# A Trainium2 decoder layer in which the sums of the second feed-forward's weight quarters are made at other places

## The chip, the cores and the metric

The kernel runs on one core of one Trainium2 chip. The metric is the time of one execution on the device in microseconds (us); lower is better. The time before is the median of three runs. A profile is one execution taken by the hardware profiler; its times count from the first instruction. The engines are TensorE (PE; PEld is its weight load), VectorE (DVE), ScalarE (ACT), GpSimd (POOL) and SyncE (SP, which here issues DMAs alone).

## The reference, cut to what matters

One layer works on x of 512 tokens by 1024, in float32. It has three steps, each with an RMS norm before and behind it and a residual.

```python
x = x + 0.5 * rms_norm(swiglu_ffn(rms_norm(x, norm_pre[0]), ffn1_w_in, ffn1_w_out), norm_post[0])
x = x + rms_norm(token_mixer(rms_norm(x, norm_pre[1]), ...), norm_post[1])
x = x + 0.5 * rms_norm(swiglu_ffn(rms_norm(x, norm_pre[2]), ffn2_w_in, ffn2_w_out), norm_post[2])

def swiglu_ffn(x, w_in, w_out):                  # w_in 1024 x 5632, w_out 2816 x 1024
    gate, up = jnp.split(x @ w_in, 2, axis=-1)
    return (jax.nn.silu(gate) * up) @ w_out
```

The token mixer projects to eight heads: four of HGRN2 (a gated linear recurrence) and four of mLSTM (scores of queries and keys under a causal mask and a decay, with a running maximum). Then it projects back.

## The kernel before, in words

**Precision.** Every large product is made of two-part numbers: a weight is cast to fp32r by ScalarE (L279, the high part), VectorE subtracts that from the weight (L281, the low part), and TensorE runs three matmuls, high by high, high by low and low by high. A split weight lies in one of four places (`WBUF`); TensorE frees a place when it has used it.

**Fewer products.** The feed-forwards use a scheme of seven products in place of eight for a 2 by 2 blocked product. It needs sums of blocks. For the input weights these are made in SBUF (L295, VectorE and some on GpSimd). For the output weights of most tiles (`QUARTERED`: eight in the first half of the output columns, five in the second, thirteen in all) the sums of a tile's quarters are made in DRAM, ahead of use, by `sums_ahead` (L862): SP copies three quarters of the weight tile into a DRAM tile (L868 to L870, 128, 128 and 256 KB), and then GpSimd issues three accumulating DMAs, DRAM to DRAM (L873): one of 256 KB, which adds the remaining quarter to two places, and two of 128 KB, each of which reads what the one before it wrote. Each waits for the landing of what it reads. The finished tile is later loaded by SP like any weight (L242, `raw<-f2sums`).

**Where the sums are made.** `sums_due` (L876) makes a list of tiles for one feed-forward and chosen halves; `make_sums` (L879) begins the next tile of the list (SP's copies) and moves every tile already begun one step on (one of GpSimd's DMAs). Calls of `make_sums` stand at fixed points of the program:

- the mixers (`mixer`, L1671): list = the eight tiles of the second feed-forward's first half. Calls: one for each of four convolution jobs (`job_f`, L1046) and one for each of eight weights of the jobs `hi` and `mv` (`job_t`, L1064). Twelve calls.
- the input products (`ffn_in`, L782): for the second feed-forward a list of five tiles (second half), one call for every tenth product from the twentieth on (`EVERY`), five calls. The first feed-forward has a list of all its thirteen tiles and a call for every fifth product, ten calls.
- the output products (`ffn_out`, L885): a call after every other tile of the first half of the columns, six in all. They begin the first feed-forward's last three tiles and finish the second's fifth.

**What sets the order.** The order of each engine's instructions is fixed when the program is built, and each engine runs its own list in order; between engines there are only semaphores. SP's copies are put behind the last weight load that was recorded before them. GpSimd's accumulating DMAs stand in GpSimd's list between its other work, and an instruction that waits for a landing holds all that is behind it on GpSimd.

**The mixers.** Long projections are cut into small jobs, and `fill(n)` puts n pieces of them between the steps of the recurrences, so that TensorE always has something. After the jobs `hi` and `mv` come `hgrn_states` (L1394) and `mlstm_scores` (L1528). For each mLSTM head, `mlstm_head` (L1504) does this: TensorE spreads a row (L1489), VectorE and ScalarE make the decay e (L1511 to L1514), GpSimd puts zeros above the diagonal (`affine_select`, L1515), TensorE makes the scores in a PSUM bank (L1523), and VectorE multiplies both into pT (L1525), which frees the bank. Before the masks, GpSimd clears a state tile C (L1548). The heads are staggered by one.

**The output products.** `ffn_out` computes the first 512 columns (half 0) with eight quartered tiles (42 matmuls, two weights each: the weight itself and its sums) and three plain ones (48 matmuls), then half 1 with five quartered tiles and six plain ones. Between the halves, `post0` takes sums of squares of half 0, on ScalarE and GpSimd (L436, L437). The last rows are normalized, added and stored (L492, L1807). The program ends with a drain on every engine and a barrier (L1861).

Of the kernel before, what the change touches and what calls it, by code (L numbers as in the profile page):

```python
# [11 lines left out]
ALU = mybir.AluOpType  # L12
# [72 lines left out]
PLACES, LATER = {2: 1, 4: 2, 6: 0, 8: 3}, {7: (2, 3)}  # L85

AGAIN, ROWS = (10,), (18, 19, 20, 21)
EVERY = 5, 10

# [25 lines left out]
class Layer:  # L117
# [663 lines left out]

    def ffn_in(self):  # L782

        self.sums_due("f2" if self.second else "f1", (1,) if self.second else (0, 1))
        for n, (p, t) in enumerate(ORDER2[len(HEADS2) :] if self.second else ORDER[len(HEADS) :]):
            if n > 14 and n % EVERY[self.second] == 0:
                self.make_sums()
            with self.behind(*(self.c22 if p == "p3" and self.second else ())):
                self.feed()
            self.c22 = []  # L790
            self.lag()
            self.prod(p, t)
            self.after(p, t)
            if t == PAIRS - 1 and p in ("p3", "p7"):
                self.hs.append(self.h_tile(len(self.hs)))
        self.feed()
        self.lag()
# [64 lines left out]
    def sums_ahead(self, f, h, k2):  # L862

        nc, to = self.nc, self.sums_of[f, h, k2]
        w = (self.ffn1_w_out, self.ffn2_w_out)[f == "f2"][0]
        q = w[k2 * 2 * P : (k2 + 1) * 2 * P, h * 512 : (h + 1) * 512].rearrange("(k p) (c f) -> p k c f", p=P, f=QUARTER)
        with self.behind(self.loaded):
            nc.sync.dma_start(to[:, 0], q[:, 0, 1])  # L868
            nc.sync.dma_start(to[:, 1], q[:, 1, 0])
            nc.sync.dma_start(to[:, 2:], q[:, 1])  # L870
        yield
        for a, b, v in ((0, 2, q[:, 0, :1].broadcast_to([P, 2, QUARTER])), (2, 3, to[:, :1]), (3, 4, to[:, 2:3])):
            nc.gpsimd.dma_start(to[:, a:b], v, accum_op=ALU.add)  # L873
            yield

    def sums_due(self, f, halves):  # L876
        self.ahead, self.making = deque(k for k in self.sums_of if k[0] == f and k[1] in halves), []

    def make_sums(self):  # L879

# [4 lines left out]
    def ffn_out(self, gpost_row, scale, after, trans, head):  # L885
# [3 lines left out]
        nc, mm = self.nc, self.nc.tensor.matmul  # L889
# [6 lines left out]
        def more(n):  # L896
            while count[0] < min(n, len(seq)):
                half, k2 = seq[count[0]]
                count[0] += 1
                if k2 in QUARTERED[half]:  # L900
                    if k2 not in kept:
                        stay = k2 in QUARTERED[1]
                        kept[k2] = self.h_quarters(k2, PLACES.get(k2)), self.h_sums(k2, stay)
                    a, f = kept[k2]
                    made.append((a, self.s_tile(f)))
                elif half and k2 in AGAIN:
                    made.append(again.popleft())
                else:
                    made.append((self.h_tile(k2, self.x_place(*LATER[k2]) if half and k2 in LATER else None), None))
                    if not half and k2 in AGAIN:  # L910
                        again.append(made[-1])
# [21 lines left out]
        def quartered(C, M, a, s, begin):  # L933

            quarter = lambda t, j: [self.quarters(t[:, b])[j] for b in range(2)]
            A, S = (lambda j: [a[0][j], a[1][j]]), (lambda j: [s[0][j], s[1][j]])
            w = self.pull()
            product(M["p1"], A(1), quarter(w, 1), begin)
            product(C[1][1], A(3), quarter(w, 3), False)
            product(C[1][0], S(3), quarter(w, 2), False)  # L940
            self.drop(w)
            v, at = self.pull(), (1, 0, 2, 3)
            product(M["p7"], S(0), quarter(v, at[0]), begin)
            product(M["p5"], S(1), quarter(v, at[1]), begin)
            product(M["p6"], S(2), quarter(v, at[2]), begin)
            product(C[0][1], A(2), quarter(v, at[3]), False)
            self.drop(v)

        def common(M, t):

            p1, q, x, y = t
            nc.scalar.copy(p1, M["p1"])
            tt(q, M["p5"], p1, ALU.subtract)
            tt(q, M["p6"], q, ALU.add)
            tt(x, q, M["p7"], ALU.subtract)
            tt(y, M["p5"], x, ALU.subtract)
            return {(1, 1): p1, (1, 0): q, (0, 0): x, (0, 1): y}

        def add(C, T, u):
            for v in range(2):  # L960
                tt(C[u][v], C[u][v], T[u, v], ALU.add)

        def pieces(C, i):
            c = slice(QUARTER * (i // 2), QUARTER * (i // 2 + 1))
            return [(C[i % 2][v][:, c], slice(QUARTER * v, QUARTER * (v + 1))) for v in range(2)]


        with self.behind(*([self.loaded] if self.second else [])):
            g = self.gain("gpost", gpost_row)
        n = 0  # L970
        for half in range(2):
            C = [[self.ps() for _ in range(2)] for _ in range(2)]
            M, T, left = None, None, len(QUARTERED[half])
            for m, k2 in enumerate(OUT[half][: PAIRS - LAST * half]):
                more(n + 2)
                h, sums = made.popleft()
                if sums:
                    begin = M is None
                    if begin:
                        M = {p: self.ps() for p in ("p1", "p5", "p7", "p6")}  # L980
                    quartered(C, M, h, sums, begin)
                    left -= 1
                    if left == 0:
                        T = common(M, [self.hf[:, j, :] for j in ROWS] if half else [self.st("c") for _ in range(4)])
                else:
                    w = self.pull()
                    more(len(seq) if half and m == PAIRS - LAST - 1 else n + 3)
                    for i in (0, 2, 1, 3):
                        for v in range(2):
                            plain(C, w, h, i, v, m == 0)  # L990
                        if i > 1 and T and m == PAIRS - 1:
                            add(C, T, i % 2)
                    self.drop(w)
                n += 1
                if half == 0 and n % 2:
                    self.make_sums()
                if n == 1:
                    self.prod("p4", PAIRS - 1)
                    self.after("p4", PAIRS - 1)
                self.lag()  # L1000
            if half == 0:
                ys = [self.post0(pieces(C, i), g, scale) for i in range(NT)]
                self.holes()
        ws = []
# [41 lines left out]
    def job_f(self, name, then):  # L1046

        w, ps = self.pull(), self.ps()
        if name[0] == "c":
            self.make_sums()  # L1050
        for k in range(ND):
            self.in_k(ps, w, k, [(0, HALF), (HALF, T)])
            if k < ND - 1:
                yield
        self.drop(w)
        then(ps)
        self.got.add(name)
        yield
# [368 lines left out]
    def job_rows(self):  # L1427

        ps = self.ps()[:100]
        for k in range(ND):  # L1430
            for n in range(2):
                for m in range(2):
                    v = slice(HALF * m, HALF * (m + 1))
                    self.nc.tensor.matmul(
                        ps[:, v], self.gw[:, k, :], self.xop(k, n, HALF * m, HALF * (m + 1)),
                        start=k + n + m == 0, stop=k == ND - 1 and n == 1, skip_group_check=True,
                    )
            if k % 2 == 1 and k < ND - 1:
                yield
        self.z = self.mb.tile([36, 2, T], F32, tag="tmp", bufs=1, name="z")  # L1440
        self.nc.scalar.copy(self.z[:, 1], ps[64:100])
        self.nc.vector.scalar_tensor_tensor(self.z[:, 0], ps[0:36], self.gb, self.z[:, 1], op0=ALU.add, op1=ALU.add)
        self.got.add("rows")
        yield
# [226 lines left out]
    def mixer(self):  # L1671
        nc, tc = self.nc, self.tc
        self.got, self.jobs = set(), deque()
        self.sums_due("f2", (0,))
        with tc.tile_pool(name="ma", bufs=1) as ma:
            self.vh = ma.tile([P, NT, NH, P], F32, name="vh")
            self.vm = ma.tile([P, NT, NH, 129], F32, name="vm")
# [187 lines left out]
```

## Time and profile before

| | us |
|---|---|
| median of three runs | 937.68 |
| lowest and highest run | 935.62, 940.22 |
| the profiled execution's time | 936.0 |
| its span, first to last instruction | 934.3 |
| TensorE busy | 922.8 |
| VectorE busy | 759.2 |
| GpSimd busy | 179.5 |

The span of 934.3 us has these stages: the first feed-forward to about 340, the mixers to about 597, the input products of the second feed-forward to 813, its output products to 927 and a tail. A row of a timeline is start, length, engine, line, operation, out<-in and, in brackets, how long the engine had been idle and what ended that. A row of a chain of waits is start, length and what the time went to. A row of windows is the stretch and its length, then for TensorE, its weight loads, VectorE, ScalarE and GpSimd the busy time (and instructions), then the granted TensorE clock, the share of the DMA engines and GB/s. A row of a DMA list is destination<-source, queue, count, size and the median time from issue to landing.

### The profile page before, as it was taken

Reading aid. Unit: us, or ns where it says so; the run is one execution under the profiler, and the core shown is the slowest. Engines: PE = TensorE matmul, PEld = TensorE weight load, DVE = VectorE, ACT = ScalarE, POOL = GpSimd, SP = SyncE. Lnnn points to the kernel's source line nnn. Section 1 sums busy time; section 2 is a strip of 40 time slices with the busy share of each in tenths; the row PEclk is TensorE's granted clock in tenths of the full one; section 3 lists DMA queues with packets and bytes.
Section 4 is the critical chain, followed back from the end, with each engine's and each line's share of the span. In section 5 each row is a group of like instructions: output and inputs, shape, how many; then the busy total and the mean of one; then the engine's idle time right before and its main releaser. Section 6 shows DMA issues by size and latency. Waiting matters only on the chain.

```text
span 934.3 us, 18295 instructions
## 1 busy us (share of the span) xinstructions
PE 922.8 (99%) x7435; PEld 887.7 (95%) x7435; DVE 759.2 (81%) x980; ACT 521.5 (56%) x751; POOL 179.5 (19%) x250
## 2 busy tenths in 40 slices
PE   9999999999999999999999999999999999999996
PEld 7999999999999999998888887899999999999996
DVE  6899988889887786698766555799899889988883
ACT  7646455557566457956523345594445545756641
POOL 3531112211111045222230310313010010100001
PEclk9999999999999999999999999999999999999999
DMA  9255778766996234477742125253376556467522
GB/s 315 70 152 143 187 206 194 193 147 160 241 276 215 81 98 123 121 176 160 170 87 63 45 90 175 88 166 93 97 192 171 150 159 198 132 193 224 175 74 91
DMA packets 116494, 142.28 MB, mean 152 GB/s; under 512 B 7189, under 2 KB 89657, under 8 KB 116410
## 3 DMA queue, kind: packets, MB, share of 16 engines
q1 hardware_dynamic: 101562, 126.95, 43.8%
q0 software_dynamic: 14560, 13.64, 11.2%
q8 instruction: 58, 0.95, 0.4%
q10 hardware_dynamic: 288, 0.52, 0.2%
q14 instruction: 26, 0.21, 0.1%
HBM read 138.99 MB, written 29.36 MB: 180 GB/s over the span
## 4 chain that ended last, share of the span: by engine, by line
PE 54%; DVE 5%; issue 2%; DMA 2%; POOL 1%; ACT 1%; DVEq 0%; POOLq 0%; ACTq 0%
PE ps L602 14%; PE ps L928 7%; PE ps L532 6%; PE ps L920 5%; PE ps L185 5%; PE ps L187 5%; PE ps L186 5%; DVE w L281 2%; PE ps L1342 2%; DMA raw<-in_ffn_w_in_dram 2%; DVE raw L295 1%; PE ps L347 1%; POOL raw L295 1%; PE ps L542 1%; PE ps L1523 0%
## 5 line engine op out<-in xcount | busy, mean ns | idle before, releaser
L279 ACT CAST w<-raw 128x1024 fp32r<-128x1024 f32 x244 | 249.6, 1029 | 195.8 <-PE ps L602 85.5
L281 DVE TENSOR_TENSOR w<-raw,w 128x1024 fp32r<-128x1024 f32 x244 | 297.5, 1222 | 32.8 <-ACT w L279 31.5
L602 PE MATMUL ps<-xq,w 128*128 128x256 f32 x2016 | 237.3, 277 | 0.0
L602 PEld LDWEIGHTS ps<-xq,w 128*128 128x128 f32 x2016 | 232.9, 188 | 0.1
L602 PE MATMUL ps<-sq,w 128*128 128x256 f32 x1512 | 178.2, 276 | 2.2 <-DVE ps L621 1.8
L602 PEld LDWEIGHTS ps<-sq,w 128*128 128x128 f32 x1512 | 174.3, 188 | 3.2 <-issue 2.0
L295 DVE TENSOR_TENSOR raw<-raw,raw 128x1024 f32<-128x1024 f32 x72 | 89.8, 1251 | 11.8 <-DMA raw<-in_ffn_w_in_dram 10.3
L920 PE MATMUL ps<-w,hs 128*128 128x256 f32 x768 | 91.2, 276 | 0.0
L920 PEld LDWEIGHTS ps<-w,hs 128*128 128x128 f32 x768 | 88.9, 188 | 0.0
L185 PE MATMUL ps<-w,xq 128*128 128x512 f32 x192 | 78.0, 407 | 0.1
L928 PE MATMUL ps<-w,hs 128*128 128x256 f32 x624 | 75.0, 276 | 0.0
L186 PE MATMUL ps<-w,xq 128*128 128x512 f32 x192 | 74.9, 391 | 0.0
L187 PE MATMUL ps<-w,xq 128*128 128x512 f32 x192 | 74.8, 391 | 0.0
L928 PEld LDWEIGHTS ps<-w,hs 128*128 128x128 f32 x624 | 72.7, 188 | 0.0
L532 PE MATMUL ps<-xq,w 128*128 128x256 f32 x480 | 55.7, 277 | 0.0
L532 PEld LDWEIGHTS ps<-xq,w 128*128 128x128 f32 x480 | 54.9, 188 | 0.5 <-issue 0.5
L814 ACT CAST hs<-hf 128x1024 fp32r<-128x1024 f32 x34 | 35.8, 1053 | 34.2 <-PE ps L928 22.3
L815 DVE TENSOR_TENSOR hs<-hf,hs 128x1024 fp32r<-128x1024 f32 x34 | 41.5, 1221 | 11.9 <-ACT hs L814 11.5
L873 POOL DMA_DIRECT2D f1sums<-f1sums x26 | 22.8, 879 | 111.7 <-DMA f1sums<-in_ffn_w_out_dram 53.1
L185 PEld LDWEIGHTS ps<-w,xq 128*128 128x128 f32 x192 | 36.1, 188 | 8.5 <-issue 0.9
L187 PEld LDWEIGHTS ps<-w,xq 128*128 128x128 f32 x192 | 36.0, 188 | 8.1 <-DVE xq L354 0.3
L873 POOL DMA_DIRECT2D f2sums<-in_ffn_w_out_dram x13 | 17.3, 1333 | 137.3 <-DMA f2sums<-in_ffn_w_out_dram 137.3
(262 smaller groups left out, 1201.6 us busy)
## 6 DMA issues: line engine op xcount, KB each, us to landing
raw<-in_ffn_w_in_dram SPq DMA_DIRECT2D x98, 512.0 KB, 4.9
raw<-in_ffn_w_out_dram SPq DMA_DIRECT2D x44, 512.0 KB, 4.5
raw<-in_w_mix_in_dram SPq DMA_DIRECT2D x28, 512.0 KB, 4.1
raw<-f1sums SPq DMA_DIRECT2D x13, 512.0 KB, 7.5
raw<-f2sums SPq DMA_DIRECT2D x13, 512.0 KB, 4.5
raw<-in_w_mix_out_dram SPq DMA_DIRECT2D x8, 512.0 KB, 4.3
f1sums<-in_ffn_w_out_dram SPq DMA_DIRECT2D x26, 128.0 KB, 4.4
f1sums<-in_ffn_w_out_dram SPq DMA_DIRECT2D x13, 256.0 KB, 5.5
```

The costliest lines, as they stand in the source:

```text
L185: mm(ps, sh, mh, start=start, stop=False, **kw)
L186: mm(ps, sh, ml, start=False, stop=False, **kw)
L187: mm(ps, sl, mh, start=False, stop=stop, **kw)
L279: nc.scalar.copy(hi, raw)
L281: self.low = nc.vector.tensor_tensor(lo, raw, hi.bitcast(F32), op=ALU.subtract)
L295: (nc.vector if late else nc.gpsimd).tensor_tensor(o, o, c, op=ALU.add)
L532: mm(ps[:, u0:u1], w[:, a, k, :], self.xop(k, b, u0, u1), start=k + n + m == 0, stop=k == ND - 1 and n == 2, skip_group_check=True,)
L602: self.nc.tensor.matmul(ps[:, c], wb[b][:, k, v], left[d][:, k, :], start=first and a + n + k == 0, stop=n == 2 and k == KH - 1, skip_grou ...
L815: self.nc.vector.tensor_tensor(lo, src, hi.bitcast(F32), op=ALU.subtract)
L873: nc.gpsimd.dma_start(to[:, a:b], v, accum_op=ALU.add)
L920: mm(out, a[kk][:, i * P : (i + 1) * P], w[:, b, kk, QUARTER * v : QUARTER * (v + 1)], start=begin and c == kk == n == 0, stop=kk == 1 and ...
L928: mm(ps[:, QUARTER * c : QUARTER * (c + 1)], A[a][:, c], B[b], start=begin and c == n == 0, stop=n == 2, skip_group_check=True,)
```

## The change

The list of the mixers gets ten tiles instead of eight (`AHEAD`), and the job of the gate rows (`job_rows`, between the convolutions and `hi`) gets a call of `make_sums` of its own, so that there are thirteen calls. The second feed-forward's input products make none. The remaining three tiles are begun in the first half of its output products, by the first three of the six calls there. Behind the last accumulating DMA a drain is issued on GpSimd. (The other edit of `job_f` names the same four jobs as before.)

```diff
-EVERY = 5, 10
+EVERY, AHEAD = 5, 10
...
     def ffn_in(self):
-        self.sums_due("f2" if self.second else "f1", (1,) if self.second else (0, 1))
+        if not self.second:
+            self.sums_due("f1")
...
-            if n > 14 and n % EVERY[self.second] == 0:
+            if n > 14 and n % EVERY == 0 and not self.second:
                 self.make_sums()
...
-            nc.gpsimd.dma_start(to[:, a:b], v, accum_op=ALU.add)
+            self.summed = nc.gpsimd.dma_start(to[:, a:b], v, accum_op=ALU.add)
...
-    def sums_due(self, f, halves):
-        self.ahead, self.making = deque(k for k in self.sums_of if k[0] == f and k[1] in halves), []
+    def sums_due(self, f, n=None, done=0):
+        self.ahead, self.making = deque([k for k in self.sums_of if k[0] == f][done:n]), []
...
     def ffn_out(self, gpost_row, scale, after, trans, head):
...
+        if self.second:
+            self.sums_due("f2", done=AHEAD)
...
             if half == 0:
+                if self.second:
+                    with self.behind(self.summed):
+                        nc.gpsimd.drain()
                 ys = [self.post0(pieces(C, i), g, scale) for i in range(NT)]
...
     def job_f(self, name, then):
-        if name[0] == "c":
+        if name in ("conv0", "conv1", "conv2", "conv3"):
             self.make_sums()
...
     def job_rows(self):
         ps = self.ps()[:100]
+        self.make_sums()
...
     def mixer(self):
-        self.sums_due("f2", (0,))
+        self.sums_due("f2", AHEAD)
```

In the built programs TensorE, VectorE and ScalarE have the same instructions in the same order before and after. On GpSimd, the six accumulating DMAs of the ninth and tenth tile stand behind those of the eighth and ahead of the clearing of C (L1548) and the four masks (L1515). Among the mixers' tiles, the sixth's first accumulation comes directly behind the fifth's, and the seventh's first one ahead of the sixth's third. The drain stands behind the last accumulating DMA and ahead of `post0`'s first instruction on GpSimd. On SP, the sixth tile's copies follow the fifth's without a weight load between, and those from the seventh to the tenth are each one weight load earlier than that count would put them; the copies of the last three tiles stand among the loads of the output weights, the first of them behind the load of the gains.

## The prediction

> **What bounds the kernel now.** Three views, in this order: the page's first part, TensorE's own waits, and the windows of single stages.
>
> ```profile
> span 934.3 us, 18295 instructions
> ...
> PE 922.8 (99%) x7435; PEld 887.7 (95%) x7435; DVE 759.2 (81%) x980; ACT 521.5 (56%) x751; POOL 179.5 (19%) x250
> ```
>
> ```profile
> PE ps L602 <- DVE ps L621: 1.8, 1, 1.8
> ```
>
> ```profile
> 753.00:775.00 22.00, 20.10 (x175) 19.74 (x174) 18.43 (x20) 8.30 (x11) 2.84 (x3) 1.00 0.66 180
> 813.00:827.00 14.00, 14.00 (x126) 14.00 (x125) 12.67 (x18) 6.14 (x10) 1.66 (x2) 1.00 0.87 224
> 827.00:870.00 43.00, 43.00 (x382) 43.00 (x381) 36.74 (x42) 27.21 (x33) 0.00 (x0) 1.00 0.64 199
> 927.20:931.00 3.80, 0.00 (x0) 0.00 (x0) 1.84 (x3) 0.31 (x2) 0.81 (x2) 1.00 0.21 78
> 931.00:934.30 3.30, 0.00 (x0) 0.00 (x0) 0.00 (x0) 0.00 (x0) 0.00 (x0) 0.51 0.18 70
> ```
>
> TensorE (first column after the length) is busy in 922.8 of 934.3 us. The profiled execution took 936.0 us, 1.7 around its span and 1.7 under the median of the runs shown (937.68); every sum below is made against 936.0. In the whole second feed-forward TensorE has one wait worth a line, 1.8 us, and the window 753 to 775 shows it: 20.10 busy of 22.00. So there is little to win, about 2 us there and something at the end of the kernel, and anything that holds TensorE in its long busy stretches costs its full length. I therefore looked for what the moved DMAs could hold up.
>
> **The change, part by part.** TensorE, VectorE and ScalarE keep their instructions in the same order. What moves is on SP (three copies per tile) and on GpSimd (three accumulating DMAs per tile).
>
> *1. Two more tiles on GpSimd's queue in the mixers.* The GpSimd timeline, with the length of the instruction and in brackets what it waited for:
>
> ```profile
> 429.87 1.49 POOL L873 DMA_DIRECT2D f2sums<-in_ffn_w_out_dram  x1
> ...
> 437.43 1.52 POOL L873 DMA_DIRECT2D f2sums<-in_ffn_w_out_dram  x1
> ...
> 445.57 0.81 POOL L873 DMA_DIRECT2D f2sums<-f2sums  x1 [4.38 <-DMA f2sums<-in_ffn_w_out_dram]
> ...
> 450.11 1.49 POOL L873 DMA_DIRECT2D f2sums<-in_ffn_w_out_dram  x1
> ...
> 463.20 1.49 POOL L873 DMA_DIRECT2D f2sums<-in_ffn_w_out_dram  x1
> ...
> 474.60 1.48 POOL L873 DMA_DIRECT2D f2sums<-in_ffn_w_out_dram  x1
> 481.00 0.85 POOL L873 DMA_DIRECT2D f2sums<-f2sums  x1 [4.92 <-DMA f2sums<-in_ffn_w_out_dram]
> 484.44 0.94 POOL L873 DMA_DIRECT2D f2sums<-f2sums  x1 [2.59 <-ACT vm L1696]
> 485.42 1.40 POOL L1548 MEMSET C<- 128x1548 f32 x1
> 486.77 0.83 POOL L1515 TENSOR_SCALAR_AFFINE_SELECT e<-e 128x512 f32<-128x512 f32 x1
> ```
>
> ```profile
> 448.01 0.49 SPq L868 DMA_DIRECT2D f2sums<-in_ffn_w_out_dram  x1
> ```
>
> ```profile
> f2sums<-in_ffn_w_out_dram POOLq DMA_DIRECT2D x13, 256.0 KB, 6.1
> f2sums<-f2sums POOLq DMA_DIRECT2D x26, 128.0 KB, 4.1
> ```
>
> SP has issued the eighth tile's copies at 448.01; GpSimd reaches that tile at 474.60. The fifth tile begins at 429.87, the sixth at 437.43. So the chain on GpSimd sets the pace: the second accumulation of a tile reads what the first wrote, the third what the second wrote, and GpSimd, in order, waits through 6.1 and 4.1 us of landing (medians of the DMA issues). Tiles begin at 450.11, 463.20 and 474.60, which is 13.1 and 11.4 us each; the last takes 9.84 from its first accumulation to its third and would free the queue after about 10.4. Behind its third accumulation, at once, stand the clearing of C and the first causal mask of the mLSTM scores (L1515): this queue is already as late as those two.
>
> The new order puts two tiles in front of them. At 11.4 and 10.4 that is 21.8 us. Something comes back: the fifth and sixth tile now issue their first accumulations together, and the seventh's goes ahead of the sixth's third, so that part of a wait such as 437.43 to 445.57 (8.1 us) lies beside another. But the same DMA engines serve both, so I take back 5.3 of the 8.1. The last third accumulation moves by 16.5, from 484.44 to 500.9. Bounds: 20.8 (twice 10.4) less the whole 8.1 gives 497.1; twice 13.1 with nothing back gives 510.6.
>
> Who waits for the mask:
>
> ```profile
> 488.60 0.68 DVE L1525 SCALAR_TENSOR_TENSOR pT<-ps,e 128x512 f32<-128x512 f32 x1
> ```
>
> ```profile
> 493.45 1.16 PE L1523 MATMUL ps<-qk 64*128 64x128 f32 x8
> ```
>
> VectorE's product pT of the first head reads the mask and frees the PSUM bank into which TensorE's third group of score products (493.45) goes. From the last third accumulation to the mask's end are 3.16 us (484.44 to 487.60); pT takes 0.68, and I allow 0.2 for two handovers: 4.04. TensorE's group can start at 500.9 + 4.04 = 504.9 instead of 493.45, and TensorE stands still for **11.5 us** (7.7 to 21.2). VectorE stands too, and with it the next splits and ScalarE's exponential of the third head, but up to four weights lie ready for TensorE, so nothing more is late when pT is done. Nothing later takes the 11.5 us back: after the start, the view of TensorE's waits has only the 1.8 us above.
>
> *2. The clock after such a gap.* After the last matmul the granted clock (third number from the end in the windows above) is still 1.00 up to 931.0 and 0.51 from there: 3.8 idle us, and it falls. At the start:
>
> ```profile
> 1.56 1.22 PE L181 MATMUL ps<-ident 128*128 128x128 f32 x4 [1.56 <-POOL ident masks.py:199]
> ...
> 6.42 1.65 PE L181 MATMUL ps<-ident 128*128 128x128 f32 x6
> 7.93 1.82 PE L347 MATMUL ps<-ident,xn 128*128 128x128 f32 x8
> 9.59 0.61 PE L181 MATMUL ps<-ident 128*128 128x128 f32 x4
> 10.07 1.32 PE L347 MATMUL ps<-ident,hf 128*128 128x128 f32 x8
> ```
>
> Six transposes from 6.42 to 7.93 are 0.25 us each, four from 9.59 to 10.07 are 0.12: half speed up to about 9.4, that is for 7.8 us from the first matmul at 1.56. A gap of 11.5 us is long enough for the clock to fall, and the way back costs between 0 and 3.9 us (half of 7.8). I take **2.0**, the middle. The Trainium skill ("TensorE: Matmul & The Clock Gate", Part 1, the HAM clock gate) says that one idle window of about 3.4 us halves the clock and about 3.4 us of work restores it; both rows agree in kind, and by its window the way back would cost 1.7 as an estimate, the sum 0.3 less.
>
> *3. No sums beside the second input products.*
>
> ```profile
> 749.31 0.51 SPq L868 DMA_DIRECT2D f2sums<-in_ffn_w_out_dram  x1
> ```
>
> ```profile
> 653.42 5.21 DMA raw<-in_ffn_w_in_dram
> ...
> 753.62 6.21 DMA raw<-in_ffn_w_in_dram
> ...
> 771.80 3.00 PE ps L602 x24
> ```
>
> ```profile
> raw<-in_ffn_w_in_dram SPq DMA_DIRECT2D x98, 512.0 KB, 4.9
> ```
>
> The chain of waits passes through a weight load of 6.21 us at 753.62, issued behind a tile's copies (749.31), and ends in TensorE's wait before 771.80. The same sort of load took 5.21 at 653.42, with no sums near, and 4.9 in the median. One us or so off the load, and less company for VectorE's next loads, takes most of the 1.8 us: **-1.5**, between 0 (VectorE is late by its own work) and -2.0. The other three tiles of this stage cost TensorE nothing now.
>
> *4. Three tiles beside the first half of the output products* in place of the end of one. The first feed-forward already runs like that:
>
> ```profile
> 240.00:283.00 43.00, 43.00 (x382) 43.00 (x381) 37.81 (x47) 27.04 (x37) 8.01 (x11) 1.00 0.95 275
> ```
>
> ```profile
> 280.60 0.81 POOL L873 DMA_DIRECT2D f1sums<-f1sums  x1 [5.91 <-DMA f1sums<-f1sums]
> 281.17 0.48 POOL L437 TENSOR_SCALAR col<-col 128x1 f32<-128x1 f32 x1
> ```
>
> There the DMA engines are 0.95 busy (0.64 in the same stage of the second, 827 to 870 above), and TensorE works 43.00 of 43.00 us. So these three tiles cost **0**; what they have taken up by then is the queue: the last accumulation is issued right ahead of the sums of squares (L437).
>
> *5. The drain.*
>
> ```profile
> L1861 POOLq DRAIN  x3: 34/102/5506, 928.0 to 934.0; - x3
> ...
> L1861 SPq DRAIN  x3: 7/7/7, 932.2 to 933.8; - x3
> ```
>
> At the end GpSimd's drain lasts 5.5 us, from 928.0 to 933.5, while SP, last of the others, is through its own at 932.2. The next drain, with no DMA between, takes 0.1. If the long one is the price of the software DMAs before it, it is now paid between the halves, and the end waits for SP: **-1.3**. If not, 0. The early one stands, by the rows of part 4, at the moment when the sums of squares are due, and can hold the two instructions of ScalarE that wait for GpSimd there, and a cast behind them, for up to 5.5 us. Up to four split weights cover that, so I cost it at 0, and at +2 if they don't.
>
> Sum: 936.0 + 11.5 + 2.0 - 1.5 + 0 - 1.3 = 946.7, about **947** (on the median of the runs it would be 948.4).
>
> **The rivals.**
>
> *A. The chain fits (not slower).* The mechanism is the same queue: if the last third accumulation is issued before 493.45 - 4.04 = 489.4, TensorE waits for nothing, and only the gains stay: 936.0 - 1.5 - 1.3 = 933.2. It needs the two tiles to cost 5.0 us net instead of 16.5, say 8.1 back and 6.5 us each. Against it: landing alone is 6.1 + 4.1 in the median, and no tile of these took under 9.8. The Trainium skill ("DMA: Bandwidth & Descriptors", Anatomy of one DMA, SWDGE path) gives about 2.0 us plus bytes over 436 GB/s, so an estimated 2.6 and 2.3 us for these two sizes, and by it the queue would be on time; the medians 6.1 and 4.1 speak against that, and these move data from HBM to HBM. Chance 0.14.
>
> *B. The drain between the halves holds TensorE.* For it: GpSimd, ScalarE's casts and TensorE hang on each other there. Against it: the cover. Price 2 to 4 us, a drain less what the cover takes: about 950. Chance 0.08.
>
> *C. The change does not bring what it is made of:* the wait before 771.80 is VectorE's own work (for it: 18.43 busy of 22.00 us from 753 to 775; against it: the load that stood before), and the last drain lasts as long as now. Then 946.7 + 2.8 = 949.5. Chance 0.10.
>
> **How the numbers follow.** The forecast has 0.68. Its own range comes from the queue's bounds, 7.7 to 21.2, of which the upper end needs the slowest tile twice: 936.0 + 7.7 - 2.0 - 1.3 = 940.4 up to about 936.0 + 17 + 2 - 1.5 = 953.5. B and C lie inside for the most part; towards A I reach down to 938. Outside is most of A and a little above 954. A measurement here tells about 0.5% (4.7 us) from no change. Faster by more than that would need more than all gains together (2.0 + 1.3): 0.04. Within it lie A and the forecast with a chain near its lower bound: 0.15. Slower: 0.81.
>
> **What would show it.** In the profile after: GpSimd's third accumulation of the tenth tile near 501 (497 to 511), the clearing of C right behind it, and a TensorE gap of some 11 us before a group of L1523, near 493, released by VectorE's L1525; a stretch under full clock behind it; no wait before the matmuls that were at 771.80 (all times there later by the gap); GpSimd's last drain short. The forecast is wrong if the clearing of C stands before 490, or if TensorE waits inside the output products.

## The result and the profile after

The kernel after takes 945.12 us (median of 6 runs, 943.48 to 949.19) beside 937.80 for the kernel before in the same sessions: a ratio of 1.0087, 95% interval [1.0068, 1.0105] (the two medians alone give 1.0078). It is slower by 7.3 us between the medians, by 8.2 by the ratio. Its profiled execution took 945.62 us, 9.6 more than that of before (936.0), and it is these 9.6 us that the traces can be asked for. The lines of the code have moved: L873 is L874 now, L1515 is L1522, L1523 is L1530, L1525 is L1532, L1548 is L1555, L1861 is L1868.

The page's first part, and TensorE's own waits:

```profile
span 943.9 us, 18290 instructions
...
PE 926.2 (98%) x7435; PEld 891.2 (94%) x7435; DVE 758.2 (80%) x980; ACT 522.1 (55%) x751; POOL 180.2 (19%) x250
```

```profile
PE ps L1530 <- DVE pT L1532: 8.5, 1, 8.5
...
PE ps L602 <- DVE ps L621: 0.7, 1, 0.7
```

One wait is new, 8.5 us before a group of score products, and the wait in the input products went from 1.8 to 0.7. GpSimd's timeline shows where the 8.5 us come from; the first row is the two first accumulations that are now issued together, the second is the eighth tile's third, and from 478.47 on it is the ninth and the tenth tile. (The two that are issued together belong to the tiles that the text above calls the fifth and the sixth. Counted in the list they are the fourth and the fifth, which changes none of the times.)

```profile
431.49 2.65 POOL L874 DMA_DIRECT2D f2sums<-in_ffn_w_out_dram  x2
...
477.94 0.81 POOL L874 DMA_DIRECT2D f2sums<-f2sums  x1 [2.67 <-DMA f2sums<-f2sums]
478.47 1.48 POOL L874 DMA_DIRECT2D f2sums<-in_ffn_w_out_dram  x1
484.54 0.85 POOL L874 DMA_DIRECT2D f2sums<-f2sums  x1 [4.59 <-issue]
487.90 0.81 POOL L874 DMA_DIRECT2D f2sums<-f2sums  x1 [2.50 <-DMA f2sums<-f2sums]
488.43 1.48 POOL L874 DMA_DIRECT2D f2sums<-in_ffn_w_out_dram  x1
495.87 0.85 POOL L874 DMA_DIRECT2D f2sums<-f2sums  x1 [5.96 <-DMA f2sums<-in_ffn_w_out_dram]
499.25 0.81 POOL L874 DMA_DIRECT2D f2sums<-f2sums  x1 [2.52 <-DMA f2sums<-f2sums]
500.10 1.39 POOL L1555 MEMSET C<- 128x1548 f32 x1
501.45 1.24 POOL L1522 TENSOR_SCALAR_AFFINE_SELECT e<-e 128x512 f32<-128x512 f32 x2
```

The rows of VectorE and TensorE that follow from the mask at 501.45, one fence for each engine:

```profile
502.14 0.69 DVE L1532 SCALAR_TENSOR_TENSOR pT<-ps,e 128x512 f32<-128x512 f32 x1 [13.82 <-POOL e L1522]
```

```profile
493.96 0.39 PE L187 MATMUL ps<-w,xq 128*128 128x512 f32 x1
502.88 2.08 PE L1530 MATMUL ps<-qk 64*128 64x128 f32 x8 [8.53 <-DVE pT L1532]
```

VectorE sat idle 13.82 us for the mask, TensorE 8.53 us for VectorE. The same eight score products took 1.16 us before and take 2.08 here: the clock has fallen. The windows of single stages (length, then TensorE, its weight loads, VectorE, ScalarE, GpSimd; granted clock, DMA share, GB/s) show that and the stages behind it:

```profile
494.35:502.88 8.53, 0.00 (x0) 0.00 (x0) 0.74 (x2) 0.00 (x0) 4.25 (x5) 0.67 0.24 33
502.88:505.50 2.62, 2.62 (x10) 2.30 (x11) 2.62 (x8) 1.57 (x2) 0.64 (x1) 0.50 0.00 0
505.50:508.00 2.50, 2.50 (x8) 2.01 (x7) 2.00 (x6) 0.73 (x2) 0.99 (x1) 0.61 0.10 11
508.00:515.00 7.00, 7.00 (x37) 5.29 (x36) 3.58 (x9) 3.12 (x6) 0.00 (x0) 1.00 0.21 72
763.00:785.00 22.00, 21.18 (x185) 20.82 (x184) 19.09 (x20) 9.00 (x11) 0.00 (x0) 1.00 0.44 137
837.00:880.00 43.00, 43.00 (x382) 43.00 (x381) 36.16 (x42) 26.86 (x31) 7.38 (x8) 1.00 0.91 263
```

TensorE's granted clock is 0.50 for 2.62 us and 0.61 in the mean of another 2.50: 2.62 x 0.50 + 2.50 x 0.39 = 2.3 us lost. From 508 on it is at full speed. In the output products it is fully busy although the DMA share there went from 0.64 to 0.91.

The drains, first those at the end, then the new one:

```profile
L1868 POOLq DRAIN  x3: 38/93/656, 938.9 to 943.6; - x3
L1868 SPq DRAIN  x3: 7/7/7, 943.1 to 943.4; - x3
```

```profile
L1007 POOLq DRAIN  x1: 6561/6561/6561, 878.0 to 878.0; - x1
```

From the start of GpSimd's last drain to the end of the span it is 943.9 - 938.9 = 5.0 us; before it was 934.3 - 928.0 = 6.3. One more difference has nothing to do with the change, the same transposes at the start of the kernel as in the rows shown of before:

```profile
9.69 1.06 PE L181 MATMUL ps<-ident 128*128 128x128 f32 x4
10.55 1.91 PE L347 MATMUL ps<-ident,hf 128*128 128x128 f32 x8
12.28 5.94 PE L602 MATMUL ps<-xq,sq 128*128 128x256 f32 x48
```

Four transposes take 1.06 us here and took 0.61, the next eight 1.91 and 1.32: in this execution the clock rose later, and what follows stands 0.8 to 0.9 us later from there on. Of the ten profiles of this case, that of before has the earliest start: the first matmul of L542, behind the first feed-forward, is at 339.73 there, at 340.56 in that of after, and between 339.94 and 341.10 in the others.

The sum of what was read: 8.5 (wait) + 2.3 (clock) - 1.1 (idle time in the input products: 1.90 of 22 us before, 0.82 here) - 1.3 (end) + 0.9 (start) = 9.3 of the 9.6 us.

### The profile page after: what moved, and what is told of

Read it like the earlier page. It is cut to its first block, busy times and chain, and to the rows that moved or that the text cites. A ratio compares the mean times of both kernels' runs of the same rounds, so it can differ in the third digit from the quotient of the medians.

```text
span 943.9 us, 18290 instructions
## 1 busy us (share of the span) xinstructions
PE 926.2 (98%) x7435; PEld 891.2 (94%) x7435; DVE 758.2 (80%) x980; ACT 522.1 (55%) x751; POOL 180.2 (19%) x250
## 4 chain that ended last, share of the span: by engine, by line
PE 36%; DVE 5%; issue 3%; DMA 3%; POOL 2%; ACT 1%; DVEq 0%; POOLq 0%; ACTq 0%
PE ps L602 13%; PE ps L929 7%; PE ps L921 5%; PE ps L185 3%; PE ps L186 3%; PE ps L187 3%; DVE w L281 2%; DMA raw<-in_ffn_w_in_dram 2%; DVE raw L295 1%; POOL raw L295 1%; DMA f2sums<-in_ffn_w_out_dram 1%; PE ps L347 1%; DVE ps L621 0%; PE ps L1642 0%; PE ps L1615 0%
## 5 line engine op out<-in xcount | busy, mean ns | idle before, releaser
L874 POOL DMA_DIRECT2D f2sums<-in_ffn_w_out_dram x13 | 18.2, 1459 | 194.6 <-DMA f2sums<-in_ffn_w_out_dram 194.6
L816 DVE TENSOR_TENSOR hs<-hf,hs 128x1024 fp32r<-128x1024 f32 x34 | 41.6, 1222 | 11.9 <-ACT hs L815 11.5
L874 POOL DMA_DIRECT2D f1sums<-f1sums x26 | 23.2, 892 | 110.8 <-DMA f1sums<-in_ffn_w_out_dram 55.5
```

What stands on the lines that cost most here:

```text
L816: self.nc.vector.tensor_tensor(lo, src, hi.bitcast(F32), op=ALU.subtract)
L874: self.summed = nc.gpsimd.dma_start(to[:, a:b], v, accum_op=ALU.add)
```

## The experiments

**Theory (the queue).** The six accumulating DMAs of the ninth and tenth tile stand ahead of the clearing of C and the causal masks on GpSimd, which goes in order; each waits for the landing of the one before it; the mask is late, VectorE's pT is late, TensorE stands still and its clock falls. The drain brings 1.3 us and the emptied input products about 1. **Rivals:** the DMAs' traffic slows the weight loads of the mixers wherever they stand (traffic); every tile in the mixers costs a share (per tile); the drain between the halves or the tiles beside the output products cost time; the gains come from something else.

Each ratio below is to runs of the kernel before on the same chip, whose median was 937.18 us for the first four kernels and 936.19 for the other four; times of different kernels are compared through it.

### Two tiles behind the masks

```diff
-        self.sums_due("f2", AHEAD)          # mixer
+        self.sums_due("f2", 8)
...
                 self.mlstm_scores(mc)
+                self.sums_due("f2", AHEAD, 8)
...
-        self.make_sums()                    # job_rows
...
-            if name in ("hi", "mv"):        # job_t
+            if name in ("hi", "mv", "hg", "mo"):
```

> The kernel after, except that the ninth and tenth tile are made behind the four causal masks: the mixers' list holds eight tiles with the twelve calls of the kernel before, and two more tiles are listed after the mLSTM scores, with calls at the weights of the jobs hg and mo. Ten tiles are still made in the mixers, none beside the second input products, three in the output products, and the drain stays. Theory (the queue): what cost time is that six accumulating DMAs stood ahead of the clearing of C and the masks. Then the wait of TensorE before its third group of score products (8.5 us in the kernel after) is gone, and the stretch at half clock behind it; what stays is the drain (-1.3) and the input products (about -1): about 935.5 us, 2.3 under the kernel before's 937.8, and some 9.6 under the kernel after's 945.1. Rival (the traffic): two more tiles' DMAs in the mixers slow the weight loads there, wherever they stand in GpSimd's queue: then about 943 to 946, with TensorE's losses spread over other waits in the mixers. A second rival: the six DMAs now hold the small GpSimd steps of the heads' norms (L338, L339), and TensorE waits there: 1 to 8 us over the theory's time, in a wait after 505 us.

Measured: 939.55 us, ratio 1.0022 [1.0008, 1.0036]: by the ratios some 6 us under the kernel after (1.0087), and 4 over the theory's time (935.5 of 937.8, a ratio of 0.9975). TensorE's waits:

```profile
PE ps L187 <- DVE xq L354: 3.2, 1, 3.2
...
PE ps L185 <- DVE y L1660: 0.8, 1, 0.8
PE ps L929 <- DVE y L474: 0.4, 1, 0.4
```

The wait before the score products is gone, so it was the place in the queue. But new ones stand behind it, as the second rival said. GpSimd's timeline of this kernel, then of the kernel before, at the last of the small steps for the heads' norms:

```profile
543.79 0.92 POOL L874 DMA_DIRECT2D f2sums<-f2sums  x1 [3.37 <-DMA f2sums<-in_ffn_w_out_dram]
...
547.85 0.90 POOL L874 DMA_DIRECT2D f2sums<-f2sums  x1 [1.75 <-DMA f2sums<-f2sums]
...
549.10 1.03 POOL L339 TENSOR_TENSOR col<-col,nhalf 128x4 f32<-128x4 f32 x1
```

```profile
541.38 1.01 POOL L339 TENSOR_TENSOR col<-col,nhalf 128x4 f32<-128x4 f32 x1
```

The last norm is made 7.7 us later, behind two accumulations that wait for landings, and 3.2 us of that reach TensorE through VectorE's y and xq. The same mechanism at another place: whatever stands behind such a chain is late. The last wait in the list (0.4) is the drain between the halves, which started at 876.7 and lasted 7.5 us.

The clock fell here too. Behind the wait of 3.2 us, which ended at 557.67, TensorE works for 3.42 us at half clock:

```profile
558.50:561.92 3.42, 3.42 (x10) 2.64 (x9) 1.56 (x3) 0.00 (x0) 0.00 (x0) 0.50 0.15 41
```

That is 1.7 us more, and with the three waits 6.1 us in this execution. It took 941.95 us, 2.4 over the median and the slowest of the twelve, so the typical loss is smaller.

### Nine tiles in front, one behind

The thirteen calls of the kernel after, a list of nine, and the tenth listed after the scores as above.

> Between the two: nine tiles ahead of the clearing of C and the masks, with the thirteen calls of the kernel after, and the tenth behind the masks as in the run before. Theory (the queue, with a threshold): the ninth tile's third accumulation was issued at 487.90 in the kernel after, under the 489.4 that the prediction gives as the latest time that costs nothing, so TensorE does not wait for the third group of score products, or under 1 us: about 935.5 us, as with eight tiles in front. Rival (each tile in front costs the same): half of the kernel after's loss, so about 940. Rival (the traffic): 943 to 946.

Measured: 937.37 us, ratio 1.0005 [0.9990, 1.0019]. No wait before the score products. GpSimd's timeline has the ninth tile's third accumulation, the clearing of C and the first mask at

```profile
486.30 0.93 POOL L874 DMA_DIRECT2D f2sums<-f2sums  x1 [2.55 <-DVE e L1520]
487.27 1.39 POOL L1555 MEMSET C<- 128x1548 f32 x1
488.62 1.25 POOL L1522 TENSOR_SCALAR_AFFINE_SELECT e<-e 128x512 f32<-128x512 f32 x2
```

and that is ahead of the 489.4 of the prediction: nine tiles in front cost nothing there. The time is nearly 3 us over the theory's 0.9975. In the profiled execution (939.25 us, 1.9 over the median) 2.1 us are again the norms, held this time by the tenth tile alone, and 1.7 are the half clock behind the longer of the two waits, which was only 1.82 us and ended at 529.10:

```profile
PE ps L185 <- DVE y L1661: 2.1, 2, 1.8
```

```profile
530.26:533.67 3.41, 3.41 (x16) 3.24 (x16) 1.63 (x5) 0.40 (x1) 1.44 (x4) 0.50 0.28 38
```

### The masks taken off GpSimd

```diff
-        nc.gpsimd.affine_select(
-            e4, e4, pattern=[[0, NT], [1, P]], compare_op=ALU.is_ge, fill=0.0, base=0, channel_multiplier=-1
-        )
+        nc.vector.tensor_tensor(e4, e4, self.tri[:, None, :].broadcast_to([P, NT, P]), op=ALU.mult)
...
+        self.tri = mc.tile([P, P], mybir.dt.bfloat16, name="tri")     # in masks
+        nc.gpsimd.memset(self.tri, 1.0)
+        nc.gpsimd.affine_select(
+            self.tri, self.tri, pattern=[[1, P]], compare_op=ALU.is_ge, fill=0.0, base=0, channel_multiplier=-1
+        )
```

> The kernel after with the same DMAs at the same places, but the four causal masks taken off GpSimd: VectorE multiplies e by a triangle of ones and zeros that GpSimd prepares once at the start of the mixers. Theory (the queue): GpSimd's third accumulation of the tenth tile still comes near 499, but nothing that TensorE needs waits behind it except the clearing of C; VectorE does four more operations of some 0.7 us each, 2.8 us in all, most of them beside TensorE's work. The 8.5 us and the half clock go: about 935.5 to 938 us. Rival: the wait of TensorE had another cause (VectorE itself, late by its own work or by the DMAs' traffic): then the gap before the third group of score products stays, and the time is 945 or more.

Measured: 934.26 us, ratio 0.9969 [0.9953, 0.9984]: faster than both kernels and a little under the 935.5 to 938 expected. GpSimd's timeline and TensorE's waits:

```profile
498.08 0.81 POOL L874 DMA_DIRECT2D f2sums<-f2sums  x1 [2.63 <-DMA f2sums<-f2sums]
498.94 1.40 POOL L1558 MEMSET C<- 128x1548 f32 x1
```

```profile
PE ps L602 <- DVE ps L621: 0.8, 1, 0.8
```

The same chain ends at nearly the same moment (498.08 beside 499.25), the same DMAs run beside the same work, and TensorE waits for none of it: it has no wait in the mixers. This settles traffic against queue: the DMAs beside the mixers cost nothing that shows, the order on GpSimd did.

### The drain alone, and the kernel after without it

The kernel before with the drain behind its last accumulating DMA; and the kernel after without the drain.

> The kernel before with nothing changed but the drain on GpSimd behind the last accumulating DMA, between the halves of the output products. Theory: the last drain of the program gets short (5.5 us before, 0.1 to 0.7 then) and SP's is what the end waits for: -1.3, so about 936.5 us; the early drain lasts 5 to 7 us and costs nothing. Rival: the early drain holds the sums of squares and with them TensorE: 2 to 4 us over the kernel before. Rival: the end does not wait for that drain: 0.

Measured: 935.89 us, ratio 0.9978 [0.9964, 0.9993]. The drains at the end, and the one between the halves:

```profile
L1864 POOLq DRAIN  x3: 34/102/656, 929.9 to 934.7; - x3
L1864 SPq DRAIN  x3: 7/7/7, 934.1 to 934.4; - x3
```

```profile
L1004 POOLq DRAIN  x1: 7359/7359/7359, 825.5 to 825.5; - x1
```

> The kernel after without the drain between the halves. Theory: the program's last drain on GpSimd is long again (about 5.5 us, as in the kernel before) and the end waits for it: +1.3 over the kernel after, so about 946.4 us; nothing changes in the output products, since the early drain cost nothing. Rival: the early drain holds TensorE between the halves and costs 2 to 4 us: then this kernel is at 942 to 944.

Measured: 945.88 us, ratio 1.0104 [1.0090, 1.0118], beside the kernel after's 1.0087 [1.0068, 1.0105].

```profile
L1865 POOLq DRAIN  x3: 38/93/5502, 937.6 to 943.6; - x3
```

From the start of GpSimd's last drain to the end of the span (935.0 and 943.9) it is 5.1 us with the early drain and 6.3 without it, 5.0 and 6.3 in the kernels after and before: the drain's 1.3 us are there in all four profiles. In the times the steps are 0.22% and 0.17%, of the same sign and with room for 1.3 us (0.14%) in their intervals, though the second pair of intervals overlaps. TensorE's wait before the score products was 7.0 us in the profile without the drain and 8.5 in the kernel after's, with the same instructions up to there: that much it varies between executions.

### The masks and the drain without the moved tiles

The kernel before with the edit of the masks and the drain.

> The kernel before with the masks on VectorE (as in the run with the masks moved) and the drain, but with the tiles of sums where the kernel before makes them: eight in the mixers, five beside the second input products. It separates what the masks on VectorE bring by themselves, and what moving the tiles brings. Theory: GpSimd held nobody with eight tiles in front, so the masks on VectorE bring nothing here: about 935.9 us, as with the drain alone. The tiles' move is then worth what the run with the masks moved (934.3) lies below that: about 1 to 1.6 us, by the wait of TensorE in the input products (1.4 to 2.0 us lost with sums beside them, 0.95 without). Rival: the masks on VectorE are what made that run fast; then this one is at 934 to 934.5 too, and the move brings nothing.

Measured: 935.95 us, ratio 0.9993 [0.9981, 1.0005]. The masks on VectorE bring nothing by themselves (the drain alone: 0.9978, 1.4 us less by the ratios, with overlapping intervals). From here to the 0.9969 with the tiles moved it is 0.24%, 2.2 us by the ratios, of which the two profiles show 0.5: TensorE's wait in the input products is 1.3 us here and 0.8 there. The move is probably worth something, but the intervals just overlap, and between 0.5 and 2.2 us these runs do not settle how much.

```profile
PE ps L602 <- DVE ps L621: 1.3, 1, 1.3
```

### Eleven tiles in front

```diff
-EVERY, AHEAD = 5, 10
+EVERY, AHEAD = 5, 11
...
-        if name in ("conv0", "conv1", "conv2", "conv3"):
+        if name in ("hq3", "conv0", "conv1", "conv2", "conv3"):
```

> Eleven tiles ahead of the clearing of C and the masks (one more call, at the last of the four HGRN query jobs; two tiles are left for the output products). Theory (the queue): with one tile more the last third accumulation comes 5 to 11 us later than the kernel after's 499.25 (it began one call earlier, which can give half a tile back), and TensorE's wait grows by as much: from 8.5 to between 13.5 and 19.5 us; what the clock costs after the gap stays at about 1.7 us, since it depends on the way back and not on the gap's length. About 951 to 956 us. Rival (the traffic, or a cost per tile of half the kernel after's loss): about 949.

Measured: 950.94 us, ratio 1.0154 [1.0140, 1.0168], by the ratios 6.3 us over the kernel after. GpSimd's third accumulation of the eleventh tile, TensorE's wait, and its windows from there:

```profile
503.23 0.81 POOL L874 DMA_DIRECT2D f2sums<-f2sums  x1 [2.53 <-DMA f2sums<-f2sums]
```

```profile
PE ps L1530 <- DVE pT L1532: 12.9, 1, 12.9
```

```profile
493.96:506.85 12.89, 0.00 (x1) 0.00 (x0) 0.74 (x2) 0.00 (x0) 5.64 (x7) 0.68 0.35 51
506.85:512.20 5.35, 5.35 (x16) 4.45 (x17) 4.63 (x12) 2.30 (x4) 1.62 (x2) 0.50 0.07 9
```

With eight and nine tiles in front TensorE waits for nothing there, with ten 8.5 us, with eleven 12.9: a threshold and then a slope. The chain ends 4.0 us later than with ten and the wait is 4.4 us longer, a little under the 5 to 11 that were expected; the time is at the lower edge of the 951 to 956 expected. That the chain began a call earlier may be the reason, but no run shows it. The clock costs 5.35 x 0.50 = 2.7 us after a gap of 12.9 and 2.3 after one of 8.5.

### Three tiles left unsummed beside the output products

The kernel with the masks on VectorE, without the nine accumulating DMAs of the last three tiles. SP's copies of these tiles stay, and the output lacks the sums.

> The kernel with the masks on VectorE and ten tiles in the mixers, with the nine accumulating DMAs of the three tiles that are made beside the output products left out (SP's copies stay; the output lacks those additions, so it is not the reference's). The drain then stands with nothing pending ahead of it, and should be short. Theory (prediction's part 4: the three tiles cost nothing in the output products): the same time, 934.3 us, within 0.5. Rival: the three tiles' traffic and the long drain in the output products cost 1 us or more there, which this kernel gains.

Measured: 935.03 us, ratio 0.9985 [0.9972, 0.9998], beside 0.9969 [0.9953, 0.9984] with them. That is 0.8 us over the 934.3 that were expected within 0.5, but the intervals overlap. It gains nothing, so those accumulations and the long drain behind them cost nothing that these runs can tell; the copies' share was not tested. The drain was not short, although that had been expected:

```profile
L1008 POOLq DRAIN  x1: 6624/6624/6624, 497.7 to 497.7; - x1
```

It stood right behind the tenth tile's last accumulation in the mixers, and there the landing was still out.

## Why the prediction was right, point by point

**1. The queue: the mechanism was right, its size too large.** 11.5 us were forecast, 8.5 were measured, inside the bounds of 7.7 to 21.2 (the 7.0 of the kernel without the drain lies just under them). The 3.0 us come from three places. The last third accumulation was issued at 499.25, not 500.9 (1.65), within the bounds of 497.1 to 510.6: the eighth tile's stands at 477.94, 6.5 us ahead of the 484.44 of before where 5.3 were taken back, and the two tiles behind it took 21.3 us, not 21.8. From there to TensorE's group it took 3.63 us (499.25 to 502.88), not 4.04 (0.4). And TensorE came to that group at 494.35, not 493.45 (0.9): the start of this execution was that much slower. With the masks off GpSimd the wait is gone and the chain is not, which shows the cause.

**2. The clock: 2.0 forecast, 2.3 measured.** The way back, from the first matmul to full speed, took from 502.88 to about 507.5 at half clock, 4.6 us, and 5.35 after the longer gap. The Trainium skill ("TensorE: Matmul & The Clock Gate", Part 1, the HAM clock gate) has about 3.4 us of work for it; these two stretches were longer, and the cost was 2.3 and 2.7 us instead of the 1.7 worked out from it. The traces show how that comes. Read in slices of half a us, the stretch at half clock, idle time included, lasts 3.41 us (one tile behind the masks), 3.42 (two behind), 6.83 (no drain), 10.24 (the kernel after, 497.23 to 507.47) and 13.65 (eleven tiles): 1, 1, 2, 3 and 4 times 3.41. So in these five traces the clock changes only in steps of 3.41 us, and it rises at the end of the first step in which TensorE worked all through. The price of a gap depends on where in a step it ends: 1.7, 1.7, 2.4, 2.3 and 2.7 us. The same section of the Trainium skill calls its window of about 3.4 us free-running, and these traces agree.

**3. No sums beside the input products: -1.5 forecast, -1.1 measured** between the two profiles. Over all ten the gain is smaller: TensorE's waits in that stage add up to 1.8, 1.4 and 1.3 us in the three kernels with sums beside it, and to between 0.5 and 1.2 in the seven without. So a wait remains without any sums near. That it is VectorE's own work, as rival C had it, is not shown.

**4. Three tiles beside the output products: 0 forecast, 0 measured.** TensorE is busy 43.00 of 43.00 us at a DMA share of 0.91, and leaving the accumulations out gains nothing that the runs can tell.

**5. The drain: -1.3 forecast, -1.3 measured** at the end, in four profiles. Between the halves it cost TensorE nothing in the kernel after, and 0.4 us in the kernel with two tiles behind the masks: rival B's mechanism exists, at a fraction of its price.

**The rivals.** A needed the third accumulation before 489.4; it came at 499.25. Its price was near all the same: in the kernel with the masks on VectorE, where nobody that TensorE needs waits behind the chain, the profiled execution took 933.53 us, and A's sum was 933.2. The landing times behind A's refusal held: the medians of the accumulating DMAs were 7.2 and 4.6 us in the kernel after, beside the 2.6 and 2.3 estimated from the Trainium skill ("DMA: Bandwidth & Descriptors", Anatomy of one DMA, SWDGE path).

```profile
f2sums<-in_ffn_w_out_dram POOLq DMA_DIRECT2D x13, 256.0 KB, 7.2
f2sums<-f2sums POOLq DMA_DIRECT2D x26, 128.0 KB, 4.6
```

Not in the sum was the start, 0.9 us later in the profiled execution of after than in that of before. So that the sum (946.7) came within 1.1 us of that execution (945.6) is in part luck: the wait was forecast 3.0 us too large, and the clock (0.3), the input products (0.4) and the start (0.9, which is also part of the 3.0) made up for 1.6 of it.

## What to carry to other kernels

A DMA that waits for another DMA's landing is cheap for the engine that issues it (0.8 to 1.5 us each here) and dear for whatever stands behind it on that engine: before such chains are moved, list what follows them in the queue and by when each is needed, and compare that with the moment when the chain's last wait ends. Up to that moment more work cost nothing here; beyond it TensorE's wait grew by about what the chain's end was later (4.4 us for 4.0), with about two microseconds of half clock on top. Where the place can't be changed, take the waiting consumer off that engine: four masks on VectorE, which gained nothing by themselves, turned a loss of 0.87% into a gain of 0.31%.

## What the runs showed of the hardware

- In these profiles a drain on GpSimd took about 5.5 us if a DMA had been issued there since the last drain, even when all of them had landed long ago: 5.506 us in the kernel before, over 100 us after its last accumulation (about 823), and 5.502 in the kernel after without the early drain, 60 us after it. Right behind such a DMA it took 6.6 to 7.5 us (8.6 with eleven tiles). With a drain between, the last one took 0.66 us although GpSimd had computed in between, and the drain at the start of the program, ahead of any DMA, took 0.17.
- The half clock after a gap cost 2.3 to 2.7 us after gaps of 7.0, 8.5 and 12.9 us, and 1.7 us even after gaps of 1.8 and 3.2 us, where the clock fell only after TensorE had begun to work again (529.10 and 530.26; 557.67 and 558.50). The gap of 1.8 us at 771.80 in the kernel before left the clock at 1.00. Which short gaps lower it, these runs do not settle.
- At the start of the kernel the same instructions reached full clock at moments that differ between the profiled executions of before and after by enough to move all that follows by 0.8 to 0.9 us, a tenth of a per cent of this kernel.
